# Where row stores, first weight splits and squares stand around a seven-product matmul stage

## The chip, the cores and the metric

The kernel runs on one core of one Trainium2 chip. The metric is device time in microseconds (us) of one execution, the median of several; a profile of one further execution goes with it. Each engine of the core works through a queue of its own in order: TensorE (PE, with its weight loads PEld), VectorE (DVE), ScalarE (ACT), GpSimd (POOL) and SyncE (SP), which here issues the transfers between main memory (DRAM) and the on-chip memory. Engines wait for each other by semaphores.

## The reference: what is computed

One layer of a bidirectional hybrid encoder for two requests with shared weights: 1024 rows of `x_sample` and 256 rows of `x_prompt`, each of width 2048.

```python
hn = rms_norm(x, norm_g)
proj = hn @ w_in                       # 2048 -> 4896 columns
xbc, z_ssd, dt_raw, q, k, v, z_att, mq, z_mem = split_cols(proj, IN_SIZES)
xbc = silu(centred_dwconv(xbc, conv_w, conv_b))          # 5 taps along the rows
...                                    # two SSD scans, windowed attention, attention to the memory
return x + concatenate([o_ssd, o_att, o_mem], axis=-1) @ w_out
```

The memory (2 x 256 rows of width 2048) is normed and multiplied with `w_mem_kv` in the same way. All matrices are float32.

## The kernel before

**Rows and places.** The 1280 rows are taken as two groups of 640; group 1 (rows 640 to 1279) comes first. A group lies transposed on the chip in 16 places, `xH0..xH15` and `xL0..xL15`, each of 128 features by 640 rows. Every float32 operand is held as two parts, a rounded one (H) and the rest (L), and a product is three matmuls: H by H, H by L, L by H. Weights come as tiles `wraw`, 128 x 512 (256 KB), and are split by `wsplit` (line 337): ACT copies the rounded part `wh`, then DVE subtracts to get `wl`. There are four buffers for `wraw` and three each for `wh` and `wl`. `wsplit` notes its two instructions in the list `marks`.

**Two kinds of block.** `block_tok` (line 367) multiplies 16 weight tiles with four or five tiles of rows and holds five sums in the `acc` banks of PSUM; its last pass takes k = 14 and 15 together, sum by sum, and calls `evac` for each (an ACT copy, then a store: `ev_raw` writes `qs`, `ev_kv` writes `kv`, the memory blocks `mkr` and `mvo`). `block_pair` (line 1326) is a Strassen-like form: seven products of half tiles stand for eight, each k having 21 matmuls of 320 columns. It needs sums of the quarters of the weight tile: `weight_sums` (line 1308) loads the tile and lets POOL make three sums `ws` in four instructions; these are split as well, into `sh` (ACT) and `sl` (DVE), three buffers each. Its seven results take the five `acc` banks and two more (`accm`).

**The order.** The blocks run as follows: the two memory blocks (MK, then MV), `q` of group 1, ten units of seven products for group 1 (`seven_stage(1)`, each unit with 8 values of k), `kv` and `q` of group 0, `seven_stage(0)`, and then the mixed part with the remaining blocks, the scans and the attention. The last part multiplies with `w_out`.

**What runs beside them.** `p_step` (line 1411) is called once for each k of a block and prepares the rows of a group by a plan written out by hand: `p_load` brings in two row tiles `ra` and `rb_`, `p_fill` (line 1378) scales them and writes the places (`xH` by ACT, `xL` by DVE), `p_sums` and `p_split` form and split the row sums `tH` and `tL`. For group 1 it runs beside MV, `q` and unit 0 of `seven_stage(1)`; for group 0 beside `kv`, `q` and unit 0 of `seven_stage(0)`. `p_fill` of group 1 also stores each place to DRAM, 32 stores `rowH` and `rowL` of 320 KB; `refill_x` reads them back in a `z1` block of the mixed part. At j = 23 and j = 25, k = 7 and 9 of the `q` block, `p_step` calls `weight_sums` for the first two weight tiles of the seven-product stage, into tiles that are free until then.

`stage_stats` (line 1513) is a generator of 48 steps, four for each group of three pieces: it loads pieces `sst` of rows (256 KB), squares and sums them on ACT, and after every fourth piece has DVE and POOL make the norm factor `rx`. It has one buffer, `xst`, which also serves for one of the first two weight tiles and for the sums `yu` of a unit. `seven_stage` (line 1665) takes one step at k = 0, 2, 4 and 5 of every unit: 40 in the first stage, 8 in the second. `some_left` and `one_left` work off the convolution of finished units (`u`, `c`).

**Who decides the order in a queue.** The framework sorts each engine's queue at build time by walking a model of the machine: whichever instruction is ready goes, and among ready ones the earlier in the program. `tc.high_priority(offset=n)` counts an instruction as standing n places earlier. `tc.issue_after(ins)` keeps those instructions of its block that go to the engine of `ins` behind `ins` in that engine's queue; it says nothing about other engines. The offsets are `HP = (30, 100, 100)`: evacuations of `block_tok` take the first, weight sums, splits and evacuations of `block_pair` the third.

```python
def wsplit(raw, h, l):
    a = A.activation(h, raw, AF.Copy)
    b = V.tensor_sub(l, raw, h.bitcast(F32))
    marks[:] = a.ins, b.ins
```

Of the kernel before, what the change touches and what calls it, by code (L numbers as in the profile page):

```python
# [10 lines left out]
F32 = mybir.dt.float32  # L11
# [10 lines left out]
KT = D // P  # L22
# [3 lines left out]
HP = (30, 100, 100)  # L26
# [124 lines left out]
def hymba_encoder_kernel(  # L151
# [79 lines left out]
    row_d = [[dram([P, 640], f"row{n}{k}") for n in "HL"] for k in range(KT)]  # L231
# [28 lines left out]
            lanes[lane].append(((fn.__name__, t), fn(t)))  # L260

    marks = []

    def step(i):
        name, gen = lanes[i][0]
# [45 lines left out]
    cur = {}  # L311
# [31 lines left out]
    def w_laid(src, n):  # L343

        def load(k, raw):
            S.dma_start(raw, src[k])
        return load, n

    def laid_in(name):
# [4 lines left out]
    def w_in_rows(name):  # L354
        return w_laid(laid_in(name), W_AT[name][1])
# [8 lines left out]
    TURNED = [4 * q + m for q in (0, 2, 1, 3) for m in range(4)]  # L364
    PAIRED = [k + 8 * i for k in range(8) for i in range(2)]

    def block_tok(w, nt, evac, before_last=None, feats=range(KT), places=range(KT)):

        load, n = w
        ps = [acc.tile([P, 512], F32, tag="acc", name="acc") for _ in range(nt)]  # L370
        hls = {}
        for k in range(KT):
            raw = wp.tile([P, 512], F32, tag="wraw", name="wraw", bufs=RB)
            load(feats[k], raw[:, :n])
            with tc.high_priority(offset=HP[2]):
                h = wp.tile([P, 512], F32R, tag="wh", name="wh", bufs=WB)
                l = wp.tile([P, 512], F32R, tag="wl", name="wl", bufs=WB)
                wsplit(raw[:, :n], h[:, :n], l[:, :n])
            hls[k] = h, l
            if k == KT - 2:  # L380
                continue
            if k == KT - 1 and before_last is not None:
                before_last(k)

            for t in range(nt):
                for k_ in ((k - 1, k) if k == KT - 1 else (k,)):
                    h, l = hls[k_]
                    sh, sl = [cur[n_, places[k_]][:, t * P:(t + 1) * P] for n_ in "HL"]
                    T.matmul(ps[t][:, :n], sh, h[:, :n], start=(k_ == 0), stop=False)
                    T.matmul(ps[t][:, :n], sh, l[:, :n], start=False, stop=False)  # L390
                    T.matmul(ps[t][:, :n], sl, h[:, :n], start=False, stop=(k_ == KT - 1))
                if k == KT - 1:
                    with tc.high_priority(offset=HP[0]):
                        evac(t, ps[t])
                if nt == 5 and t < 4:
                    yield 0.4 if k == KT - 1 else 0.2
            if k == KT - 1:
                yield k - 1
            yield k
# [908 lines left out]
    def weight_sums(src, i):  # L1308

        if i >= 8 * src.shape[0]:  # L1310
            return
        if i < 2 and src is w_in_pairs:
            raw = fin.tile([P, 512], F32, tag=("xst", "tL7")[i], name="wraw0")
        else:
            raw = wp.tile([P, 512], F32, tag="wraw", name="wraw", bufs=RB)
        S.dma_start(raw, src[i // 8, i % 8])
        with tc.high_priority(offset=HP[2]):
            sums = fin.tile([P, 384], F32, tag="ws", name="ws", bufs=3)
            w11, w12, w22, w21 = [raw[:, i * P:(i + 1) * P] for i in range(4)]
            s1, s2, s4 = [sums[:, i * P:(i + 1) * P] for i in range(3)]  # L1320
            for o, x, y, op in ((s1, w21, w22, ALU.add), (w21, w11, w21, ALU.subtract),
                                (s2, s1, w11, ALU.subtract), (s4, w12, s2, ALU.subtract)):
                G.tensor_tensor(out=o, in0=x, in1=y, op=op)
        ahead.append((raw, sums))

    def block_pair(src, u, rows_of, begin, lead=1):

        ps = {p: (acc.tile([P, 512], F32, tag="acc", name="acc") if i < 5 else psum("accm"))[:, :320]
              for i, p in enumerate(seven)}
        parts = {}  # L1330
        for k in range(8):
            weight_sums(src, 8 * u + k + lead)
            with tc.high_priority(offset=HP[2]):
                raw, sums = ahead.pop(0)
                h = [wp.tile([P, 512], F32R, tag="wh", name="wh", bufs=WB),
                     fin.tile([P, 384], F32R, tag="sh", name="sh", bufs=3)]
                l = [wp.tile([P, 512], F32R, tag="wl", name="wl", bufs=WB),
                     fin.tile([P, 384], F32R, tag="sl", name="sl", bufs=3)]
                wsplit(raw, h[0], l[0])
                wsplit(sums, h[1], l[1])  # L1340
            parts[k] = h, l
            if k == 2:
                evac = begin(u)
            if k == 6:
                continue
            ks = (6, 7) if k == 7 else (k,)
            for p, (i, m, c) in seven.items():
                for k_ in ks:
                    h, l = [x[i][:, m * P:(m + 1) * P] for x in parts[k_]]
                    xh, xl = rows_of(k_, p, c)  # L1350
                    T.matmul(ps[p], h, xh, start=(k_ == 0), stop=False)
                    T.matmul(ps[p], h, xl, start=False, stop=False)
                    T.matmul(ps[p], l, xh, start=False, stop=(k_ == 7))
                if k == 7:
                    with tc.high_priority(offset=HP[2]):
                        evac(p, ps[p])
            yield k
# [20 lines left out]
    def p_fill(k, grp):  # L1378

        for i, x in enumerate(raw[k]):  # L1380
            g_ = R_G + k + 8 * i
            V.scalar_tensor_tensor(out=x, in0=x, scalar=vec[:, g_:g_ + 1], in1=rbc, op0=ALU.mult, op1=ALU.mult)
            h, l = new_place(k + 8 * i)
            A.activation(h, x, AF.Copy)
            V.tensor_sub(l, x, h.bitcast(F32))
            if grp == 1:
                for d, y in zip(row_d[k + 8 * i], (h, l)):
                    S.dma_start(d, y.bitcast(F32))

    def p_sums(k):  # L1390
        a, b = [hv(x, 2) for x in raw[k]]
# [19 lines left out]
    def p_step(j, grp):  # L1411
        if j == (3, 9)[grp]:
            need(x_rows, [1 - grp])
        if j in (23, 25):
            weight_sums(w_in_pairs, (j - 23) // 2)
        with ExitStack() as st:
            for ins in marks:
                st.enter_context(tc.issue_after(ins))
            for f, k, *args in sorted(p_plan[grp].get(j, ()),
                                      key=lambda x: ((p_split, p_sums, p_fill, p_load).index(x[0]), x[1])):  # L1420
                f(k, *args)
# [99 lines left out]
    def run(gen, rates, after=None, hold=0, lag=2, extra=None):  # L1521

        begun, fine = 0, False
        for k in gen:
            if isinstance(k, float):
                fine = True
                if begun >= hold:
                    pump(part_of(rates, k))
                continue
            begun = k + 1  # L1530
            if after is not None and k % 4 == 3:
                pend.extend(after(k // 4))
            if hold:
                for _ in range(2 if k < KT - 4 else 0):
                    if pend:
                        u = pend.popleft()()
                        next(u)
                        next(u)
            else:

                if loaded and (len(loaded) == lag or not pend or k >= KT - 4):
                    next(loaded.popleft())
                if pend and k < KT - 4:
                    loaded.append(pend.popleft()())
                    next(loaded[-1])

            if k >= hold:
                pump(part_of(rates, 0.2 if fine else 1.0))
            if extra is not None:
                extra(k)  # L1550
# [103 lines left out]

    def tok(name, evac, rates=(0, 0), after=None, extra=None, paired=False):
        order = PAIRED if paired else range(KT)
        run(block_tok(w_in_rows(name), 5, evac, feats=order, places=order), rates, after, extra=extra)

    queue(0, vectors, [0])
    tok("q", ev_raw(q_d, 5), (1.0, 0), extra=lambda k: p_step(16 + k, 1), paired=True)  # L1660
# [4 lines left out]
    def seven_stage(grp):  # L1665
        owe = 0.0
        for u, unit in enumerate(units):
            for k in block_pair(w_in_pairs, u, rows_in, ev_seven(*unit, grp), lead=2):
                if k in (0, 2, 4, 5):
                    next(squares, None)  # L1670
                owe = owe + 1.15 if left else 0.0
                while owe >= 1:
                    owe -= 1
                    one_left()
                if u == 0:
                    p_step(32 + k, grp)

    def both(k, j):
        one_left()
# [180 lines left out]
```

## Time and profile before

| what | value |
|---|---|
| median of 3 runs | 1792.16 us (1790.08 to 1795.26) |
| profiled execution | 1788.47 us, its span 1786.8 us |
| PE busy | 1762.2 us, 99% of the span |
| DVE, ACT, POOL busy | 1302.3, 974.9, 668.4 us |
| moved by DMA | 313.23 MB, 175 GB/s on average |
| granted TensorE clock, mean | 0.998 |

The span runs from the first to the last instruction of the program. A row of a timeline has the start in us, the duration in us, the engine, the source line (here always that of a helper), the operation with its output and inputs, the count, and in brackets the idle time of the engine before it with what ended it. A row of the table by windows has, for each engine, the busy time and in brackets the number of instructions, then the granted clock (1.00 is full), the share of time in which the DMA engines were busy, and GB/s. Matmuls overlap, so a matmul's duration is longer than the distance from its start to the next one's start; that distance is what the array needs.

### The profile page before, as it was taken

To read this page: it belongs to the slowest core of one execution; us is meant where nothing else is said; L and a number is where in the kernel's file an instruction comes from. 1 tells how busy PE (TensorE), PEld (TensorE's weight loads), DVE (VectorE), ACT (ScalarE), POOL (GpSimd) and SP (SyncE) were. 2 spreads that over 40 slices of the span, in tenths; PEclk is the share of its full clock that TensorE was granted. 3 is DMA by queue.
4 is the path that set the end of the run, shared out by engine and by line. 5 is a ranking of instruction groups with operands and counts; after the bars stand their busy time and mean duration, and the time that the engine had idled before them with its cause. 6 is when DMAs were issued, how large, how long until landed. Compare 5 with 4: busy or idle time off the path is not lost.

```text
span 1786.8 us, 30971 instructions
## 1 busy us (share of the span) xinstructions
PE 1762.2 (99%) x10306; PEld 1574.1 (88%) x10306; DVE 1302.3 (73%) x2417; ACT 974.9 (55%) x2181; POOL 668.4 (37%) x1092
## 2 busy tenths in 40 slices
PE   9999999999999999999999999999999999999999
PEld 7778999999799999988778877877788888889999
DVE  5585788888958888787788777768776533766665
ACT  6554545554454444346778766657886533433433
POOL 0105788970158889421111001121110100058775
PEclk9999999999999999999999999999999999999999
DMA  8795454455443333366557876666885635644442
GB/s 297 236 309 177 140 140 144 127 146 180 146 148 106 103 118 109 100 200 199 155 162 243 258 248 185 218 199 221 249 254 164 207 115 149 209 136 147 148 142 78
DMA packets 210993, 313.23 MB, mean 175 GB/s; under 512 B 21584, under 2 KB 84368, under 8 KB 210832
## 3 DMA queue, kind: packets, MB, share of 16 engines
q1 hardware_dynamic: 210688, 311.19, 56.1%
q8 instruction: 81, 1.33, 0.3%
q14 instruction: 80, 0.66, 0.1%
q10 hardware_dynamic: 144, 0.06, 0.0%
HBM read 242.42 MB, written 68.75 MB: 174 GB/s over the span
## 4 chain that ended last, share of the span: by engine, by line
PE 81%; issue 6%; DMA 5%; DVE 4%; ACT 2%; POOL 1%; SPq 0%; DVEq 0%; ACTq 0%; POOLq 0%
PE acc L128 58%; PE accm L128 11%; PE py L128 2%; PE psc L128 1%; PE po L128 1%; DVE wl L128 1%; PE pst L128 1%; PE ppt L128 1%; DMA rf<-ac 1%; PE pmo L128 1%; PE pms L128 1%; PE pyf L128 1%; PE pyb L128 1%; DMA wraw<-in_w_in_pairs_dram 1%; DMA rb<-ac 0%
## 5 line engine op out<-in xcount | busy, mean ns | idle before, releaser
L128 PE MATMUL acc<-wh,xH 128*128 128x512 f32 (+1 forms) x1248 | 490.7, 394 | 4.2 <-ACT wh L128 3.7
L128 DVE TENSOR_TENSOR wl<-wraw,wh 128x512 fp32r<-128x512 f32 (+1 forms) x480 | 353.1, 740 | 173.9 <-ACT wh L128 169.8
L128 PE MATMUL acc<-wl,xH 128*128 128x512 f32 (+1 forms) x1248 | 475.1, 381 | 2.8 <-DVE wl L128 2.6
L128 PE MATMUL acc<-wh,xL 128*128 128x512 f32 (+1 forms) x1248 | 472.6, 379 | 0.0
L128 ACT ACTIVATE wh<-wraw 128x512 fp32r<-128x512 f32 (+1 forms) x480 | 291.7, 614 | 200.4 <-PE acc L128 125.7
L128 POOL TENSOR_TENSOR ws<-wraw 128x128 f32<-128x128 f32 x224 | 144.7, 646 | 400.4 <-DMA wraw<-in_w_in_pairs_dram 202.9
L128 PEld LDWEIGHTS acc<-wh,xH 128*128 128x128 f32 x1248 | 234.9, 188 | 51.1 <-issue 7.0
L128 PEld LDWEIGHTS acc<-wl,xH 128*128 128x128 f32 x1248 | 235.2, 188 | 48.7 <-issue 6.5
L128 PEld LDWEIGHTS acc<-wh,xL 128*128 128x128 f32 x1248 | 234.6, 188 | 44.5 <-issue 1.0
L128 ACT ACTIVATE sh<-ws 128x384 fp32r<-128x384 f32 x224 | 116.3, 524 | 275.6 <-POOL ws L128 132.3
L128 DVE TENSOR_TENSOR sl<-ws,sh 128x384 fp32r<-128x384 f32 x224 | 157.1, 704 | 136.8 <-ACT sh L128 134.8
L128 POOL TENSOR_TENSOR ws<-wraw,ws 128x128 f32<-128x128 f32 x224 | 153.4, 685 | 17.3
L128 POOL TENSOR_TENSOR ws<-ws,wraw 128x128 f32<-128x128 f32 x224 | 152.8, 682 | 0.0
L128 POOL TENSOR_TENSOR wraw<-wraw 128x128 f32<-128x128 f32 x224 | 134.9, 602 | 17.3
L128 PE MATMUL acc<-xH,wl 128*128 128x320 f32 x320 | 100.1, 313 | 1.7 <-DVE wl L128 1.4
L128 PE MATMUL acc<-tH,sh 128*128 128x320 f32 x320 | 99.1, 310 | 1.9 <-ACT qs L128 1.9
L128 PE MATMUL acc<-tH,sl 128*128 128x320 f32 x320 | 99.2, 310 | 0.0
L128 PE MATMUL acc<-xL,wh 128*128 128x320 f32 x320 | 98.9, 309 | 0.0
L128 PE MATMUL accm<-tH,wl 128*128 128x320 f32 x320 | 98.8, 309 | 0.0
L128 PE MATMUL acc<-xH,wh 128*128 128x320 f32 x320 | 98.7, 309 | 0.0
L128 PE MATMUL accm<-tL,wh 128*128 128x320 f32 x320 | 98.7, 308 | 0.0
L128 PE MATMUL accm<-tH,wh 128*128 128x320 f32 x320 | 98.7, 308 | 0.0
(458 smaller groups left out, 3833.0 us busy)
## 6 DMA issues: line engine op xcount, KB each, us to landing
wraw<-in_w_in_pairs_dram SPq DMA_DIRECT2D x160, 256.0 KB, 2.7
wraw<-in_w_in_laid_dram SPq DMA_DIRECT2D x128, 256.0 KB, 3.6
wraw<-in_w_out_laid_dram SPq DMA_DIRECT2D x64, 256.0 KB, 3.0
wraw<-in_w_out_pairs_dram SPq DMA_DIRECT2D x64, 256.0 KB, 2.9
rf<-ac SPq DMA_DIRECT2D x40, 256.0 KB, 3.8
rb<-ac SPq DMA_DIRECT2D x40, 256.0 KB, 4.1
wraw<-in_w_mem_laid_dram SPq DMA_DIRECT2D x32, 256.0 KB, 4.4
ra<-in_x_turned_dram SPq DMA_DIRECT2D x16, 320.0 KB, 3.2
```

Of the source, the lines that this page charges most:

```text
L128: r = f(*a, **kw)
```

## The change

Five things are edited.

1. `p_fill` no longer stores the places. A new function `keep_rows` issues one store; `seven_stage(1)` calls it at k = 0, 2, 4 and 7 of units 2 to 9, 32 times in all.
2. The loads and sums of the first two weight tiles, called at j = 23 and 25, stand in a block that queues their load behind the load of the weight tile last asked for (`raws[0]`).
3. In unit 0 of a stage the splits of k = 0, 1 and 2 (`wh`, `wl`, `sh`, `sl`) are queued on ACT and DVE behind the last split of the block in front.
4. `stage_stats` takes no step in unit 0 of either stage: 36 steps in the first stage, 12 in the second.
5. Evacuations of the blocks with `paired=True` (the two `q` blocks and the `kv` block between the seven-product stages) have the offset 100 in place of 30.

```diff
@@ step / w_laid @@
+    raws = [None]
...
-            S.dma_start(raw, src[k])
+            raws[0] = S.dma_start(raw, src[k]).ins
@@ block_tok @@
-                    with tc.high_priority(offset=HP[0]):
+                    with tc.high_priority(offset=rush):
@@ block_pair @@
+        front = tuple(marks) if u == 0 else ()
         for k in range(8):
             weight_sums(src, 8 * u + k + lead)
-            with tc.high_priority(offset=HP[2]):
+            with ExitStack() as st:
+                st.enter_context(tc.high_priority(offset=HP[2]))
+                for ins in front if k < 3 else ():
+                    st.enter_context(tc.issue_after(ins))
@@ p_fill @@
-            if grp == 1:
-                for d, y in zip(row_d[k + 8 * i], (h, l)):
-                    S.dma_start(d, y.bitcast(F32))
@@ p_step @@
-        if j in (23, 25):
-            weight_sums(w_in_pairs, (j - 23) // 2)
         with ExitStack() as st:
             for ins in marks:
                 st.enter_context(tc.issue_after(ins))
+            if j in (23, 25):
+                st.enter_context(tc.issue_after(raws[0]))
+                weight_sums(w_in_pairs, (j - 23) // 2)
@@ tok @@
-        run(block_tok(..., feats=order, places=order), rates, after, extra=extra)
+        run(block_tok(..., feats=order, places=order, rush=HP[2 * paired]), rates, after, extra=extra)
@@ seven_stage @@
-                if k in (0, 2, 4, 5):
+                if k in (0, 2, 4, 5) and u:
                     next(squares, None)
+                if grp == 1 and 2 <= u < 10 and k in (0, 2, 4, 7):
+                    keep_rows(4 * (u - 2) + (0, 2, 4, 7).index(k))
...
+    def keep_rows(i):
+        with ExitStack() as st:
+            for ins in marks:
+                st.enter_context(tc.issue_after(ins))
+            k, n = divmod(i, 2)
+            S.dma_start(row_d[k][n], cur["HL"[n], k].bitcast(F32))
```

More of the change, by code (lines that the diff above doesn't have):

```diff
@@ L365, in hymba_encoder_kernel, with block_tok @@
     PAIRED = [k + 8 * i for k in range(8) for i in range(2)]
-    def block_tok(w, nt, evac, before_last=None, feats=range(KT), places=range(KT)):
+    def block_tok(w, nt, evac, before_last=None, rush=HP[0], feats=range(KT), places=range(KT)):
         load, n = w
@@ L1656, in tok @@
         order = PAIRED if paired else range(KT)
-        run(block_tok(w_in_rows(name), 5, evac, feats=order, places=order), rates, after, extra=extra)
+        run(block_tok(w_in_rows(name), 5, evac, feats=order, places=order, rush=HP[2 * paired]), rates, after, extra=extra)
     queue(0, vectors, [0])
```

## The prediction

> **What bounds the kernel now.** First the page: which engine is busy throughout, and what the chain that ended last is made of. Then a table by windows of the places that the change touches, and last the timelines of single engines there.
>
> ```profile
> span 1786.8 us, 30971 instructions
> PE 1762.2 (99%) x10306; PEld 1574.1 (88%) x10306; DVE 1302.3 (73%) x2417; ACT 974.9 (55%) x2181; POOL 668.4 (37%) x1092
> ...
> PE 81%; issue 6%; DMA 5%; DVE 4%; ACT 2%; POOL 1%; SPq 0%; DVEq 0%; ACTq 0%; POOLq 0%
> ```
>
> PE is the bound. Work taken from another engine gains nothing; only places where PE stands still, or runs slowly, can be won. They show where a window holds fewer matmuls than an undisturbed one:
>
> ```profile
> 48.00:58.00 10.00, 8.66 (x37) 6.63 (x36) 3.79 (x5) 4.35 (x9) 4.23 (x8) 1.00 0.80 254
> 106.00:116.00 10.00, 8.53 (x38) 6.75 (x37) 5.96 (x10) 3.09 (x5) 0.00 (x0) 1.00 0.98 348
> 153.00:163.00 10.00, 8.02 (x41) 7.24 (x41) 3.92 (x7) 5.16 (x12) 2.56 (x7) 0.83 0.71 234
> 272.00:282.00 10.00, 8.63 (x59) 8.37 (x58) 9.79 (x15) 4.05 (x9) 9.45 (x14) 1.00 0.43 133
> 484.00:499.00 15.00, 12.68 (x49) 9.84 (x49) 6.84 (x10) 7.62 (x15) 8.05 (x12) 0.89 0.38 111
> 300.00:400.00 100.00, 99.67 (x681) 99.40 (x680) 86.72 (x143) 52.89 (x106) 86.93 (x131) 1.00 0.47 134
> 455.00:485.00 30.00, 30.00 (x134) 24.82 (x133) 28.09 (x47) 14.99 (x25) 2.72 (x4) 1.00 0.53 155
> ```
>
> The last two give the undisturbed distances: 100/681 = 0.147 us for 320 columns, 30/134 = 0.224 us for 512. Against them the others lose:
> - A, MK to MV (48:58): 10 - 37 x 0.224 = 1.7 us
> - B, inside `q` of group 1 (106:116): 10 - 38 x 0.224 = 1.5
> - C, `q` to `seven_stage(1)` (153:163; three of the 41 are of 512): 10 - 3 x 0.224 - 38 x 0.147 = 3.7
> - D, inside `seven_stage(1)` (272:282): 10 - 59 x 0.147 = 1.3
> - F, end of `q` of group 0 (484:499): 15 - 49 x 0.224 = 4.0
>
> A, B, C and F sum to 10.9 us. 0.3% of 1792.16 is 5.4 us, about what a measurement of this kernel can tell from no change, so the change can be seen only if it wins half of this.
>
> **Part 4, squares out of unit 0 (C).** In these timelines the bracket is the idle time before the instruction and who ended it.
>
> ```profile
> 149.82 1.06 ACT L128 ACTIVATE qs<-acc 128x512 f32<-128x512 f32 x2
> 155.15 0.63 ACT L128 ACTIVATE sst<-sst 128x512 f32<-128x512 f32 x1 [4.26 <-DMA sst<-in_x_sample_dram]
> 155.77 1.07 ACT L128 ACTIVATE qs<-acc 128x512 f32<-128x512 f32 x2
> 156.73 1.15 ACT L128 ACTIVATE wh<-wraw 128x512 fp32r<-128x512 f32 x2
> ...
> 154.25 0.31 PE L128 MATMUL acc<-xH,wl 128*128 128x320 f32 x1
> 156.40 0.55 PE L128 MATMUL acc<-tH,sh 128*128 128x320 f32 x1 [1.85 <-ACT qs L128]
> 156.75 0.47 PE L128 MATMUL acc<-tL,sh 128*128 128x320 f32 x1
> 157.02 0.47 PE L128 MATMUL acc<-tH,sl 128*128 128x320 f32 x1
> ```
>
> ACT has evacuated two sums of `q`; next in its queue is a square whose piece is still on its way. ACT stands for 4.26 us, behind it stand the evacuations that free the `acc` banks, and PE waits 1.85 us for one. Afterwards the matmuls start 0.27 us apart (156.75 to 157.02) and the clock of the window is 0.83: 3.7 - 1.85 = 1.85 us more. Without the square, the third evacuation comes at about 150.9 in place of 155.77, ahead of 154.25. Each step taken out of unit 0 is one 256 KB load, one square with its read-out and, every fourth, a reduction and two POOL instructions; all run later in the same stages under busy PE (the second stage gets 12 in place of 8): nothing. Next in line are `wh` and `wl` of k = 1, which need buffers that `q` frees at its end; PE needs them 21 x 0.147 = 3.1 us later, and a split takes 0.6 on ACT and about as much on DVE. I take all of C: 3.7.
>
> **Parts 2 and 3, first sums and splits behind the block in front (A and F).** SP and ACT around A, ACT and POOL around F:
>
> ```profile
> 41.02 0.33 SPq L128 DMA_DIRECT2D dtb<-in_dt_bias_dram  x1
> ...
> 44.45 0.43 SPq L128 DMA_DIRECT2D wraw<-in_w_in_pairs_dram  x1
> ...
> 52.00 0.53 ACT L128 ACTIVATE sh<-ws 128x384 fp32r<-128x384 f32 x1 [2.94 <-POOL ws L128]
> 52.43 1.14 ACT L128 ACTIVATE wh<-wraw 128x512 fp32r<-128x512 f32 x2
> ...
> 53.09 0.50 PE L128 MATMUL acc<-wh,xH 128*128 128x512 f32 x1 [0.65 <-ACT wh L128]
> 54.28 0.50 PE L128 MATMUL acc<-wl,xH 128*128 128x512 f32 x1 [0.69 <-DVE wl L128]
> ...
> 480.85 0.91 POOL L128 TENSOR_TENSOR ws<-wraw 128x128 f32<-128x128 f32 x1 [67.37 <-DMA wraw<-in_w_in_pairs_dram]
> ...
> 483.76 0.53 ACT L128 ACTIVATE sh<-ws 128x384 fp32r<-128x384 f32 x1 [3.28 <-POOL ws L128]
> ...
> 488.59 0.74 ACT L128 ACTIVATE tH<-rb__5692 128x640 fp32r<-128x640 f32 x1 [2.52 <-DVE rb__5692 L128]
> 489.23 1.14 ACT L128 ACTIVATE wh<-wraw 128x512 fp32r<-128x512 f32 x2
> ...
> 489.90 0.50 PE L128 MATMUL acc<-wh,xH 128*128 128x512 f32 x1 [1.62 <-ACT wh L128]
> 491.11 0.79 PE L128 MATMUL acc<-wl,xH 128*128 128x512 f32 x1 [0.70 <-DVE wl L128]
> ```
>
> At 44.45 SP loads a weight tile of the stage that begins shortly before 154.25, and at 52.00 ACT makes its `sh`, having stood 2.94 us for POOL's sums; the `wh` of MV behind it is what PE waits for. At 483.76 it is `sh` of k = 2 that stands ahead of the last `wh` of `q` and holds ACT for 3.28 us, and PE waits 1.62 and 0.70 us for `wh` and `wl`. The edit keeps these splits of k = 0 to 2 behind the last split of the block in front, so neither can precede that `wh`. I take A and F whole: 1.7 + 4.0. Their work is then due between the last split and the stage (at F from 489.23 to about 499). For k = 0 and 1 that is two `sh` on ACT (2 x 0.53), two `sl` on DVE and eight POOL instructions, one weight load each on SP behind the load of k = 7. They are covered by the ACT idle time above (4.26 at C, 2.52 at F). Uncovered, two `sh` and two `sl` at about 0.8 are 1.1 + 1.6 = 2.7 us at each of the two borders. Between 0 and 5.4 I take 2.0 given back, nearer to 0 because the idle rows stand beside it.
>
> **Part 1, the stores.** SP and ACT ahead of B:
>
> ```profile
> 78.31 0.33 SPq L128 DMA_DIRECT2D rowH<-xH  x1
> ...
> 102.30 0.33 SPq L128 DMA_DIRECT2D rowH<-xH  x1
> ...
> 105.25 0.32 SPq L128 DMA_DIRECT2D rowH<-xH  x1
> 106.11 0.32 SPq L128 DMA_DIRECT2D rowL<-xL  x1
> 106.48 0.42 SPq L128 DMA_DIRECT2D rb__1225<-in_x_turned_dram  x1
> 106.96 0.96 SPq L128 DMA_DIRECT2D wraw<-in_w_in_laid_dram  x1
> ...
> 111.71 0.63 ACT L128 ACTIVATE wh<-wraw 128x512 fp32r<-128x512 f32 x1 [3.19 <-DMA wraw<-in_w_in_laid_dram]
> ```
>
> A weight load stands behind stores that wait for `xH` and `xL`, with the DMA engines 98% busy in that window, and `wh` comes late. If the stores are gone, so is B; but the two row loads between them wait for buffers too. Between 0 and 1.5 I take half: 0.75. In their new place 32 stores of 320 KB share SP with the weight loads:
>
> ```profile
> wraw<-in_w_in_pairs_dram SPq DMA_DIRECT2D x60, 256.0 KB, 2.7
> ...
> wraw<-in_w_in_laid_dram SPq DMA_DIRECT2D x16, 256.0 KB, 3.9
> ```
>
> The first row is from 200 to 400 us, the second from 77 to 145, where the stores are now: a weight load beside stores lands 1.2 us later. From nothing to 32 x 1.2 = 38 us, I take nothing: in 300:400 the DMA engines are 47% busy and POOL, next after the load, 87%, so a landed tile stands in POOL's queue.
>
> **Part 5, evacuations.** Where `kv` meets `q`, PE waits this long for an evacuation that stands behind a split:
>
> ```profile
> PE acc L128 <- ACT kv L128: 0.4, 1, 0.4
> ```
>
> From 0 to 0.4, I take 0.2. At C and F the new offset only puts evacuations level with the splits; it is counted there.
>
> **The sum.** 1.7 + 0.75 + 3.7 + 4.0 + 0.2 - 2.0 = 8.35 us. The profiled execution took 1788.47 us, 1.67 over its span, and would take 1780.1; the median of the runs shown is 3.7 us above it, so 1792.16 - 8.35 = 1783.8. Its own range: 1780 (all of B, nothing given back) to 1787.2 (5.4 given back).
>
> **A rule weighed.** After C's wait of 1.85 us the clock row is 0.83, after F's two waits 0.89, after A's two of 0.65 and 0.69 it is 1.00: the slow stretch goes with the longer waits. [...]
>
> **Rivals.**
> - *Only the waits are won.* The slow stretch at a stage's start stays for a reason of its own. Then C gives 1.85 and F 2.32 in place of 7.7: 8.35 - 3.5 = 4.85 us, 1787.3. For it: both slow stretches lie at a border. Against it: in the border at A the clock held.
> - *The stores do not move.* `issue_after` in `keep_rows` names instructions of ACT and DVE, the store is SP's, and SP's queue is sorted by readiness: `dtb` above is loaded at 41.02, though its step stands in the `q` block, all of MV later. The first row is ready by 78.31. Then B stays and stage 1 is free of stores: 1783.8 + 0.75 = 1784.6.
> - *The border stays crowded.* Splits and evacuations, all at offset 100, meet on ACT in that time; 2.7 us come on PE's path at both borders and bring the slow stretch of about 1.85 each: what is won before anything is given back, 8.35 + 2.0 = 10.35 us, shrinks by 2 x 4.55 to 1.25, 1790.9.
> - *Slower: stores in front of weight loads.* In units 2 to 9 every store delays a load, POOL's sums and PE. D shows the chain: POOL is busy for 9.45 of 10 us there and PE loses 1.3 us. With 10.35 us won elsewhere, it decides from 10.35/32 = 0.32 us a store; at 0.5 us, under half of the 1.2 above, 16 - 10.35 = 5.65 slower, 1797.8.
>
> **How the numbers follow.** Forecast 0.38, stores not moved 0.25, crowded 0.20, slower 0.09, only waits 0.08. Forecast and unmoved stores lie below 1786.8, nearly all faster by over 0.3%: 0.61 with their upper edge and a few of the others set off. Crowded and only-waits are within 0.3%, with that edge 0.30; slower 0.09. The range drops the slower case and reaches to the crowded one, 1791; downward it takes D as well (1.3) and the runs' own spread of about 2 us below a median: 1777.
>
> **What would show it.** In the changed trace: no `sh` on ACT before the last `wh` of `q`; no idle ACT for `sst` between evacuations at C; PE without waits at 52, 154 and 488 and the clock 1.00 there; `rowH` and `rowL` on SP between 200 and 405 if they moved, between 78 and 145 if not. The prediction is wrong if a new PE wait for `qs`, `wh` or `sl` stands at a border, or if waits for `sh` or `sl` follow stores inside the stage.

## The result, and the profile after

The changed kernel takes 1774.85 us (median of 4 runs, 1773.83 to 1778.13) against 1792.94 for the kernel before on the same chip: a ratio of 0.9903, interval 0.9883 to 0.9923. A second comparison gave 1776.25 against 1790.24, 0.9921 (0.9909 to 0.9934). The change is faster by 0.8 to 1.0%, 14 to 18 us. The forecast was 1783.8 with a range from 1777 to 1791: the sign was right, the gain was 1.7 to 2.2 times the 8.35 us of the sum, and the time lies below the range in both comparisons.

The page of the profile after (profiled execution 1773.83 us):

```profile
span 1772.1 us, 30974 instructions
PE 1755.3 (99%) x10306; PEld 1572.0 (89%) x10306; DVE 1310.9 (74%) x2417; ACT 971.8 (55%) x2181; POOL 683.8 (39%) x1092
...
PE 88%; DMA 4%; DVE 3%; ACT 2%; issue 1%; POOL 1%; SPq 0%; ACTq 0%; DVEq 0%; POOLq 0%
```

The span is 14.7 us shorter with the same 10306 matmuls. In the chain that ended last PE has 88% where it had 81%, and "issue" 1% where it had 6%: PE stands still less often. The table by windows shows where. The borders here are the first matmuls of the blocks; the rows are the memory blocks with `q` of group 1, `seven_stage(1)`, `q` of group 0, and the mixed part. Before:

```profile
5.40:153.50 148.10, 144.96 (x636) 118.32 (x635) 95.18 (x152) 79.56 (x147) 16.50 (x31) 1.00 0.82 275
153.50:405.80 252.30, 248.62 (x1682) 247.24 (x1681) 202.64 (x331) 129.53 (x260) 204.15 (x314) 0.99 0.48 140
...
439.10:498.70 59.60, 56.90 (x243) 46.09 (x242) 48.95 (x76) 30.45 (x50) 10.77 (x16) 0.97 0.56 166
...
777.80:1583.90 806.10, 798.40 (x4230) 651.90 (x4229) 572.01 (x1251) 515.50 (x1325) 88.10 (x164) 1.00 0.64 199
```

After:

```profile
5.40:149.00 143.60, 143.50 (x636) 118.34 (x635) 96.90 (x152) 81.51 (x150) 25.62 (x34) 1.00 0.85 289
149.00:396.10 247.10, 246.44 (x1681) 245.90 (x1680) 203.22 (x330) 125.96 (x252) 201.96 (x309) 1.00 0.47 137
...
428.80:483.20 54.40, 54.40 (x242) 45.06 (x241) 52.82 (x78) 30.11 (x50) 19.78 (x22) 1.00 0.58 179
...
762.60:1570.00 807.40, 798.21 (x4231) 652.21 (x4230) 572.82 (x1252) 514.06 (x1325) 87.82 (x164) 1.00 0.64 199
```

The second number of a row is the length of the block. The first block lost 4.5 us, the first stage 5.2, the `q` block of group 0 5.2; `kv` ahead of it (33.3 to 32.7 between these borders) 0.6. All that comes later is 0.8 us longer in sum (the mixed part alone 1.3). The windows of 10 us at the five places A, B, C, D and F, each shifted about as far as its block (the last is 15 us):

```profile
48.00:58.00 10.00, 10.00 (x46) 8.29 (x45) 2.15 (x4) 4.91 (x12) 0.74 (x2) 1.00 0.81 262
106.00:116.00 10.00, 10.00 (x46) 8.29 (x45) 10.00 (x15) 5.56 (x10) 9.77 (x7) 1.00 0.94 316
149.00:159.00 10.00, 10.00 (x70) 9.99 (x69) 8.46 (x13) 5.96 (x11) 5.28 (x8) 1.00 0.37 116
267.00:277.00 10.00, 9.96 (x68) 9.97 (x69) 9.46 (x15) 5.40 (x11) 9.45 (x15) 1.00 0.41 104
468.50:483.50 15.00, 15.00 (x68) 12.44 (x67) 13.14 (x18) 8.57 (x15) 10.62 (x15) 1.00 0.38 125
```

A holds 46 matmuls in place of 37 (9 x 0.224 = 2.0 us), B 46 in place of 38 (1.8 us), C none too few, D 68 in place of 59 (9 x 0.147 = 1.3 us), F 68 in place of 49 (19 x 0.224 = 4.3 us). The granted clock is 1.00 in all five. All five losses are gone, D among them, which the forecast had left standing, and no new one stands beside them.

One thing did not happen: the stores did not move. Transfers issued by SP between 77 and 145 us in the kernel after, with the time from issue to landing:

```profile
rowH<-xH SPq DMA_DIRECT2D x15, 320.0 KB, 4.5
rowL<-xL SPq DMA_DIRECT2D x15, 320.0 KB, 4.9
```

The other two lie just outside this window; from 185 to 400 us there is none. What changed is the order in SP's queue (timeline of SP after):

```profile
97.50 0.38 SPq L128 DMA_DIRECT2D ra<-in_x_turned_dram  x1
98.18 0.33 SPq L128 DMA_DIRECT2D rb__1209<-in_x_turned_dram  x1
98.56 2.14 SPq L128 DMA_DIRECT2D wraw<-in_w_in_laid_dram  x3
100.75 0.44 SPq L128 DMA_DIRECT2D wraw<-in_w_in_pairs_dram  x1
101.23 0.43 SPq L128 DMA_DIRECT2D rowL<-xL  x1
```

Row loads and weight loads now stand ahead of a store that once stood ahead of them. What that saves shows in the waits of SP's queue from 77 to 145 us (total, times, longest). Before:

```profile
SPq L128 <- ACT xH L128: 17.0, 13, 2.2
SPq L128 <- DVE xL L128: 6.4, 13, 0.9
```

After:

```profile
SPq L128 <- DVE wl L128: 13.3, 14, 1.6
...
SPq L128 <- ACT xH L128: 1.1, 2, 0.7
```

For 23.4 us SP stood before a store whose `xH` or `xL` was not written yet, with loads behind it, some of which could have gone: for the weight load at 106.96 us, the one that B waits for, the buffers were free by 102.17 us, when DVE's last split before B ended. Now that is 1.1 us. SP waits for `wl` instead (13.3 us in place of 3.2), that is for a free `wraw` buffer, and for `tL` (10.1 in place of 4.4), that is for a free row buffer: the loads are as far ahead as the buffers allow.

### The profile page after: what moved, and what is told of

It is laid out like the page before. It is cut to its first block, busy times and chain, and to the rows that moved or that the text cites. A ratio compares the mean times of both kernels' runs of the same rounds, so it can differ in the third digit from the quotient of the medians.

```text
span 1772.1 us, 30974 instructions
## 1 busy us (share of the span) xinstructions
PE 1755.3 (99%) x10306; PEld 1572.0 (89%) x10306; DVE 1310.9 (74%) x2417; ACT 971.8 (55%) x2181; POOL 683.8 (39%) x1092
## 4 chain that ended last, share of the span: by engine, by line
PE 88%; DMA 4%; DVE 3%; ACT 2%; issue 1%; POOL 1%; SPq 0%; ACTq 0%; DVEq 0%; POOLq 0%
PE acc L128 66%; PE accm L128 11%; PE py L128 2%; PE po L128 1%; PE psc L128 1%; PE pst L128 1%; PE pmo L128 1%; PE pms L128 1%; PE ppt L128 1%; DMA wraw<-in_w_in_laid_dram 1%; PE pyf L128 1%; DMA xst<-in_x_prompt_dram 1%; DVE wl L128 1%; PE pyb L128 0%; ACT lg L128 0%
## 5 line engine op out<-in xcount | busy, mean ns | idle before, releaser
L128 POOL TENSOR_TENSOR ws<-wraw 128x128 f32<-128x128 f32 x224 | 156.9, 700 | 365.8 <-DMA wraw<-in_w_in_pairs_dram 163.1
L128 DVE TENSOR_TENSOR sl<-ws,sh 128x384 fp32r<-128x384 f32 x224 | 158.7, 712 | 115.4 <-ACT sh L128 113.9
L128 POOL TENSOR_TENSOR wraw<-wraw 128x128 f32<-128x128 f32 x224 | 139.8, 624 | 17.1
```

Of the source, the lines that this page charges most:

```text
L128: r = f(*a, **kw)
```

## The experiments

Parts are numbered as in the change. Ratios are against the kernel before, on the same chip.

**Parts 2 and 3 alone.** The kernel before with `weight_sums` of j = 23 and 25 behind `raws[0]`, and the splits of k < 3 of unit 0 behind `marks`.

> Before with parts 2 and 3 alone (first two weight loads behind the block's loads, splits of k = 0 to 2 behind the last split of the block in front). Border theory (each part takes away the waits of its own border, and the parts add up): the waits at 52 us (A) and 488 us (F) go with the slow stretch after F, 1.9 + 4.4 = 6.3 us less than before; the wait at 154 us (C) and that at 111 us (B) stay. Rival 'queue order on SP' (the gain is the row stores' lower rank behind weight loads): under 2 us. Rival 'crowded border': the splits that now come late take the place of the waits, under 3 us, with PE waits for sh, sl or wh at 154 and 498.

1783.62 us, 0.9966 (0.9953 to 0.998). The waits for `wh` and `wl` at A and F are gone but for 0.2 us; but from 100 to 160 us PE waits more than before:

```profile
PE acc L128 <- ACT wh L128: 2.9, 3, 1.8
PE acc L128 <- ACT qs L128: 1.2, 2, 0.8
PE acc L128 <- DVE wl L128: 0.5, 2, 0.2
```

The two loads of the seven-product weights are now late in the `q` block, in a queue that still stands before the stores. From 100 to 150 us PE does 201 matmuls, against 214 before and 224 with the whole change: parts 2 and 3 without part 1 cost 13 x 0.224 = 2.9 us there. At the second border, where the kernel before has no wait for `qs`, there is one now (470 to 500 us):

```profile
PE acc L128 <- ACT qs L128: 1.1, 2, 0.8
```

With F gone PE comes to this border earlier, and ACT stands 1.42 us for the piece of a square with two evacuations behind it; in the kernel before it stood 0.33 us there.

**Part 4 alone.** The kernel before with no step of `stage_stats` in unit 0:

```diff
-                if k in (0, 2, 4, 5):
+                if k in (0, 2, 4, 5) and u:
```

> Before with part 4 alone (no step of the squares in unit 0). Border theory: the wait at 154 us (C) and its slow stretch go, 3.9 us less than before; A, B and F stay. Rival 'queue order on SP': nothing. Rival 'next in line' (wh or sh of unit 0 is late as well): under 1.5 us, with a PE wait for wl or sl shortly after 154.

1788.97 us, 0.9992 (0.9979 to 1.0004). C is gone. What is left of the PE waits from 100 to 160 us is B, in the profiled execution longer than before (2.0 us in place of 1.5) and with a slow stretch behind it (clock 0.83 from 113.9 to 123.9 us), so that little gain is left: the median is 1.9 us lower, and the interval takes in no change.

**Part 1 alone.** The kernel before with the stores out of `p_fill` and `keep_rows` in the stage.

> Before with part 1 alone (the stores in keep_rows). In the changed kernel's trace the stores are issued from 76 to 140 us, as before from 78 to 141, only behind more of the weight loads. Border theory: only B goes, 1.8 us less than before, and the stores are issued up to about 141 us here too. Rival 'queue order on SP': with the weight loads in front, the waits of the memory and q blocks and some of those at the borders go, 5 us or more.

1783.61 us, 0.9969 (0.9956 to 0.9983). The stores again go out from 79 to 139 us, and the view of waits has not one row for PE from 100 to 160 us: B is gone, and so is C, although the squares are where they were. ACT at the border:

```profile
148.35 0.60 ACT L128 ACTIVATE qs<-acc 128x512 f32<-128x512 f32 x1 [0.76 <-PE acc L128]
150.42 0.63 ACT L128 ACTIVATE sst<-sst 128x512 f32<-128x512 f32 x1 [1.48 <-DMA sst<-in_x_sample_dram]
...
151.05 1.07 ACT L128 ACTIVATE qs<-acc 128x512 f32<-128x512 f32 x2
```

The square still stands ahead of two evacuations, but its piece arrives after 1.48 us of idle ACT and not after 4.26.

**Part 5 alone.** `block_tok` with `rush=HP[2 * paired]`, else the kernel before.

> Before with part 5 alone (evacuations of the paired blocks at offset 100). Border theory: only the wait of 0.4 us for an evacuation between kv and q goes, 0 to 0.7 us less than before. Rival: the evacuations now pass the square at 154 us (C) on ACT as well, 3.9 us less, and part 4 is not needed.

1791.9 us, 1.0007 (0.9997 to 1.0017): only the wait of 0.4 us for `kv` at the start of `q` of group 0 was at stake. It is gone, which cannot be measured in the time. At C the square still comes first on ACT (4.15 us idle), and waits of 1.4 us for `qs` are left.

**The change without part 1.** The stores back in `p_fill`.

> The changed kernel with part 1 undone: p_fill stores the places again. Theory 'rank' (the stores stay beside the q block and only stand behind the weight loads in SP's queue, which spares q of group 1 its waits for wh): 4 to 6 us slower than the changed kernel, about 1780 beside a before of 1791, with PE waits for wh between 105 and 150. Theory 'border' of the prediction: 1.8 us slower, one wait near 111.

1783.21 us, 0.9957 (0.9945 to 0.9969). The block of memory and `q` takes 149.15 us, 5.5 more than with part 1, the first stage 249.14, 2.0 more:

```profile
5.40:154.55 149.15, 145.68 (x636) 118.58 (x635) 97.47 (x151) 79.48 (x147) 19.51 (x32) 1.00 0.80 276
154.55:403.69 249.14, 247.24 (x1682) 245.97 (x1680) 203.95 (x331) 127.58 (x255) 204.30 (x311) 1.00 0.44 137
```

Within the whole change part 1 is worth 7.5 us by these two rows, 6.4 or 9.7 us by the ratios (0.9957 against 0.9921 or 0.9903, of 1791 us): about half of the gain, ten times the term of the forecast. Not all of this was there in the kernel before: from 100 to 150 us PE does 201 matmuls here as with parts 2 and 3 alone, so that 2.9 us of the loss come only with parts 2 and 3, most likely by part 2's loads in the same queue.

**The change without part 4, and without parts 2 and 3.** In each the named parts are undone.

> The changed kernel with part 4 undone: four steps of the squares in unit 0 of either stage. With part 1 alone the wait at 154 was gone although the squares stayed. Theory 'the squares matter only while the stores hold up SP': within 1 us of the changed kernel. Theory 'border': 3.9 us slower, a PE wait for qs at the start of the stage.

1776.45 us, 0.9917 (0.9904 to 0.993), as with part 4: with parts 1 and 5 there it adds nothing that can be measured.

> The changed kernel with parts 2 and 3 undone. Theory 'border': A and F come back, with A's 2.3 and F's 2.0 of waits in the traces of the kernels that lack these parts: 4.3 us slower than the changed kernel, and up to 6.5 where the slow clock follows F. Rival 'the other parts cover it': under 2 us.

1785.97 us, 0.9972 (0.9963 to 0.9981). Within the change parts 2 and 3 are thus worth 9.1 or 12.4 us (against 0.9921 or 0.9903), more than the 4.3 to 6.5 expected and no less than part 1. A and F are back, with their waits and, at F, the slow stretch (matmuls 0.42 us apart where 0.227 is the undisturbed distance); the profile is of the slowest run, 1790.52 us:

```profile
53.90 0.51 PE L128 MATMUL acc<-wh,xH 128*128 128x512 f32 x1 [1.46 <-ACT wh L128]
55.10 0.50 PE L128 MATMUL acc<-wl,xH 128*128 128x512 f32 x1 [0.70 <-DVE wl L128]
...
483.61 0.50 PE L128 MATMUL acc<-wh,xH 128*128 128x512 f32 x1 [1.95 <-ACT wh L128]
484.81 0.79 PE L128 MATMUL acc<-wl,xH 128*128 128x512 f32 x1 [0.71 <-DVE wl L128]
485.41 0.63 PE L128 MATMUL acc<-wh,xL 128*128 128x512 f32 x1
485.83 0.63 PE L128 MATMUL acc<-wh,xH 128*128 128x512 f32 x1
```

**Part 2 undone, part 5 undone, and the change once more.**

> The changed kernel with part 2 undone: the first two weight tiles of the stage are loaded and summed as early as before (44 to 55 us), part 3 still keeps their splits late. Theory 'splits': A and F came from the splits alone, so this is within 1 us of the changed kernel. Rival 'loads': the early loads or POOL's sums were part of A, 1 to 2 us slower, with a PE wait near 52.

1777.37 us, 0.9927 (0.9914 to 0.994). A and F stay away: the splits alone (part 3) remove them, and the interval overlaps with the change's, so that part 2 adds nothing that can be measured. One wait of 0.9 us for `wh` is new in MV.

> The changed kernel with part 5 undone (evacuations of the paired blocks at offset 30). Theory 'border': with parts 2 and 3 alone PE waited 1.2 and 1.1 us for qs at the two borders; either of parts 4 and 5 may have taken that away. If part 5 did: 1.5 to 2.5 us slower than the changed kernel, with waits for qs and kv. If part 4 did: within 1 us.

1775.77 us, 0.9919 (0.9906 to 0.9932), no different from the change.

> The changed kernel once more, beside the others on one chip: ratio 0.990 (0.988 to 0.992), the clock 1.0 or 0.999 in every run, a spread under 5 us. Theory 'slow clock' (before loses some 2 to 7 us a run to slow stretches that follow its waits, by chance of the moment): the runs of before lie the higher the lower their clock, about 1.6 us for each 0.001.

1776.25 us, the second comparison above.

**Is it the place of the stores?** The changed kernel, with each store of `keep_rows` also queued on SP behind the pair load last issued:

```diff
-        S.dma_start(raw, src[i // 8, i % 8])
+        pairs[0] = S.dma_start(raw, src[i // 8, i % 8]).ins
...
+            st.enter_context(tc.issue_after(pairs[0]))
             k, n = divmod(i, 2)
```

> The changed kernel with each store of keep_rows queued on SP behind the pair load last issued in the program, so that the stores really go out in units 2 to 9. Theory 'rank': the q block is already free of waits, so nothing more is won: within 1 us of the changed kernel, stores between 200 and 400 us. Rival 'stores in front of weight loads' (the prediction's slower case): a store holds up a weight load, POOL's sums and PE, 0.3 us each or more: 5 to 16 us slower, PE waits for sl or wl in the stage. Rival 'less traffic in q': 1 to 2 us faster.

Now the stores did move, to 190 to 379 us. The time is 1774.46 us, 0.9909 (0.9894 to 0.9923): the same. Windows of the `q` block and of the stage in this kernel:

```profile
100.00:150.00 50.00, 50.00 (x224) 41.50 (x223) 41.54 (x64) 24.22 (x40) 19.46 (x24) 1.00 0.51 158
200.00:380.00 180.00, 179.29 (x1220) 178.35 (x1219) 156.83 (x248) 93.67 (x189) 161.02 (x239) 1.00 0.62 196
```

and in the changed kernel:

```profile
100.00:150.00 50.00, 50.00 (x224) 41.54 (x224) 41.62 (x63) 24.27 (x41) 21.74 (x24) 1.00 0.90 315
200.00:380.00 180.00, 179.34 (x1223) 178.81 (x1222) 155.67 (x248) 93.82 (x189) 159.94 (x239) 1.00 0.50 144
```

The DMA engines go from 90% to 51% busy beside `q` and from 50% to 62% in the stage, and PE does the same 224 matmuls in the one and, within 3, as many in the other. Neither the traffic beside `q` nor the stores beside the stage's weight loads cost PE anything that these counts or the time show.

**Is it the rank?** The change without part 1, with the stores in `p_fill`, but the weight loads of the paired blocks given an earlier rank; then the row loads as well:

```diff
-            load(feats[k], raw[:, :n])
+            with tc.high_priority(offset=400 if rush == HP[2] else 0):
+                load(feats[k], raw[:, :n])
@@ p_load, second kernel only @@
-            S.dma_start(raw[k][i], x_turned[grp, r * P:(r + 1) * P, :])
+            with tc.high_priority(offset=400):
+                S.dma_start(raw[k][i], x_turned[grp, r * P:(r + 1) * P, :])
```

> The changed kernel with part 1 undone (p_fill stores the places) but the weight loads of the q and kv blocks counted as 400 places earlier. The stores keep their place and their amount; only the rank of the weight loads in SP's queue is raised. Theory 'rank': the waits between 105 and 150 us go as with keep_rows, ratio about 0.991, 1 to 2 us from the changed kernel. Rival 'traffic' (the 10 MB of stores beside the loads are what costs): as with part 1 undone, ratio 0.9957, waits for wh near 109 and 142.

1782.5 us, 0.9954 (0.9942 to 0.9967). From 100 to 150 us PE does 220 matmuls, against 201 without the new rank: 4.3 us won there, and no wait for `wh` is left. SP's waits for `xH` and `xL` are still 17.1 us, and the row loads still stand behind stores; waits for `qs` came back, 1.6 us in two.

The whole time did not follow the 4.3 us: it is that of the change without part 1, and the rival 'traffic' had forecast this ratio. In the profile 1.8 went in the mixed part, whose program is the same. So this run bears the rank out for the waits for `wh`, not for the whole price.

> As loads_first (stores in p_fill, parts 2 to 5 as in the changed kernel), with the row loads of p_load counted 400 places earlier too. Theory 'rank': SP's waits for xH no longer hold up anything, ratio 0.990 to 0.992 as in the changed kernel, no PE wait between 100 and 155. Rival 'traffic': the stores' amount beside the loads costs, ratio stays at 0.995.

1782.5 us, 0.9947 (0.9934 to 0.996). From 100 to 170 and from 470 to 500 us no PE wait is left, with the stores where they were before the change, the DMA engines 94% busy, more than in any other kernel here, and SP's waits for `xH` and `xL` down to 3.1 us:

```profile
100.00:150.00 50.00, 50.00 (x222) 41.41 (x221) 40.75 (x67) 23.34 (x39) 5.31 (x11) 1.00 0.94 327
```

For the waits that is rank, not traffic. The time missed its expectation and is where the rival had it. The trace shows a reason that the edit itself made: row loads now also pass the weight loads of MK, ACT stands 8.15 us for a weight tile there, and PE waits.

```profile
35.41 0.79 PE L128 MATMUL acc<-wh,xH 128*128 128x512 f32 x1 [2.28 <-ACT wh L128]
```

```profile
36.00:46.00 10.00, 10.00 (x32) 7.88 (x32) 3.01 (x6) 5.48 (x14) 0.76 (x2) 0.70 0.71 220
```

With the window ahead of it (26:36, 33 matmuls) that is 65 matmuls in 20 us where the changed kernel has 92: 27 x 0.224 = 6.0 us of the 7.5 that part 1 is worth: the edit moved the loss to the front. A wait of 1.4 us for `kv` at 440 us is new too. That the time would be the changed kernel's without these two is worked out from the trace; no run shows it. (The first stage, 247.49 us between its borders, is as short as with the change.)

**Do parts 4 and 5 cover each other?** The change with both undone.

> The changed kernel with parts 4 and 5 both undone. Theory 'either covers the other': one of them alone was enough at the borders, without both PE waits for qs at 150 and 484, 1 us each as with parts 2 and 3 alone, ratio 0.993 to 0.995. Rival 'neither is needed once the stores no longer hold up SP': ratio 0.990 to 0.992.

1778.38 us, 0.9928 (0.9913 to 0.9944). Waits for `qs` are back at both borders; the rows are from 100 to 170 us and from 470 to 500 us:

```profile
PE acc L128 <- ACT qs L128: 0.6, 1, 0.6
...
PE acc L128 <- ACT qs L128: 1.1, 2, 0.8
```

Undoing part 4 alone left 0.3 us of them at the second border, undoing part 5 alone left none. The intervals of the ratios overlap with the change's, so that the cover shows in the waits, not in the time.

## Why the prediction was wrong

| step | forecast, us | profile after, us |
|---|---|---|
| A, MK to MV | 1.7 | 2.0 |
| B, inside `q` of group 1 | 0.75 | 1.8 |
| rest of memory and `q` | 0 | 0.7 |
| C, start of `seven_stage(1)` | 3.7 | 3.9 |
| D and the rest of the stage | 0 | 1.3 |
| `kv` to `q`, and F | 0.2 + 4.0 | 0.6 + 5.2 |
| given back at the two borders | -2.0 | 0 |
| all later blocks | 0 | -0.8 |
| sum | 8.35 | 14.7 |

The sum fell 6.35 us short of the 14.7 in the profile (C is what the first stage won less D). The step that failed is the sizing of the sum's terms; the places and most of the mechanism were right. Most went wrong at four terms: 2.0 us were to be given back and none were; B and the rest of its block, priced at 0.75, held 2.5; `kv` to F held 5.8 in place of 4.2; and D, 1.3 us, was left standing. A and C held 0.5 more, and the later blocks cost 0.8. The median fell 2.7 us further: the forecast kept the 3.7 us by which the median of the kernel before stood above its profiled execution, and after the change that distance is 1.0 us (1774.85 against 1773.83). Which run is profiled is chance; that slow stretches behind waits are gone (the mean granted clock is 0.999 or 1.0 in the four runs after, and went from 0.996 to 0.999 in 27 runs of the kernel before) would make the distance smaller too, but this is not shown apart. The sum's own lower edge, given as 1780, is 1781.1 by its terms (1792.16 - 8.35 - 0.75 - 2.0), still above the result.

*Part 1: the term that failed most, by parts.* The prediction saw the mechanism (a weight load behind stores that wait for `xH`) and priced it at the one PE wait it could see, half of 1.5 us. Done alone, it gains 5.6 us by its ratio (0.9969); undone, it costs about 7.5, 2.9 of them by way of parts 2 and 3. A queue that stands for 23.4 of 68 us delays other loads too, and the delay shows at another place under another name: the pieces `sst` come later (4.26 us of idle ACT in place of 1.48), and C is a wait for `qs` behind the late square. The rival "the stores do not move" was right about the place, and right about why: `issue_after` on ACT's and DVE's instructions binds nothing on SP. Its price was wrong ("then B stays"): a store that is asked for later loses its rank to loads that are ready, and that was enough to free PE of its waits: with part 1 alone SP's waits for `xH` and `xL` fell from 23.4 to 7.2 us, and PE has none from 100 to 160 us.

*Part 4: right place, but not part 4's alone.* C has two sufficient removals: without the square (part 4 alone) or with its piece in time (part 1 alone). In the full change either would do. Its 3.7 us were rightly counted once, but neither part can be credited with them, and this swap between parts did not move the sum.

*Parts 2 and 3: right place, too small.* A and F were to be won whole, and were; undone, they come back. Part 3 alone does it. With 1.7 + 4.0 won and 2.0 given back they were to bring 3.7 us net; by place A and `kv` to F brought 7.8, and undoing them costs 9.1 or more. Parts 2 and 3 without part 1 leave waits of 4.6 us from 100 to 160 us, where the kernel before has 3.4. The product of the four ratios of single parts is 0.9966 x 0.9992 x 0.9969 x 1.0007 = 0.9934, against 0.9903 and 0.9921 for the whole: the parts seem to help each other, but the intervals touch, so that this is only indicated.

*The 2.0 us given back did not come,* and the rival of the crowded border is refuted for the whole change. With parts 2 and 3 alone waits for `qs` of 1.2 and 1.1 us stood at the two borders, the second of them new, and with parts 4 and 5 undone 0.6 and 1.1: what the term feared was there, but as late evacuations, and either of parts 4 and 5 takes away nearly all of it, which the sum did not count. The late splits themselves cost nothing that the trace shows: the three `sh` fit between the last splits of `q`, where ACT was idle before and after them (timeline of ACT after):

```profile
139.00 0.63 ACT L128 ACTIVATE wh<-wraw 128x512 fp32r<-128x512 f32 x1 [2.72 <-PE acc L128]
139.54 1.34 ACT L128 ACTIVATE sh<-ws 128x384 fp32r<-128x384 f32 x3
142.40 0.63 ACT L128 ACTIVATE wh<-wraw 128x512 fp32r<-128x512 f32 x1 [1.52 <-PE acc L128]
```

*The slower rival fell by the run with moved stores:* 32 of them beside the stage's weight loads left 0.7 us of PE waits from 150 to 400 us, as many as in the changed kernel. *Only the waits are won* fell too: with the waits gone, the clock is 1.00 at C and F.

*Open:* D, 1.3 us, which no step of the prediction touched, went away as well, and this was luck. From 200 to 380 us PE does 1215 matmuls before and 1223 after, but 1222 with part 4 alone, 1224 without parts 2 and 3, and 1212 without part 5, whose time is the change's; no part can be credited, and no run isolates why. Nor is it explained why the mixed part, the same program in all, varies from 805 to 811 us over the profiles. A kernel without any row stores was not tried, since the mixed part reads them back.

## What to carry to other kernels

When an in-order queue issues both loads and stores, read its own waits first: price a store by the time the queue stands before it for its producer and by everything queued behind, not by the one PE wait beside it (here 23.4 of 68 us against a wait of 1.5). To defer a store, it was enough here to let it be asked for later than the loads that could go (23.4 us of SP's waits became 7.2 with part 1 alone); check in the queue's timeline where it really went, since an ordering on another engine's instruction bound nothing here: 30 of the 32 stores went out between 77 and 145 us, ahead of the stage that calls for them. And if a loss has two sufficient removals, undo each part of the change by itself before crediting either.

## What the hardware showed that was not expected

Slow stretches of the array (at F in the kernel before, matmuls 0.42 us apart in place of 0.227) came after waits shorter than the stretch (at C 1.85 us, then 3.5 us from 156.40 to 159.92), and the length of the wait alone did not decide. After 1.85 us (C) the clock of the window was 0.83, after 2.28 us (all loads first) 0.70; after 1.79 us in the kernel with parts 2 and 3 alone it stayed full:

```profile
143.50:153.50 10.00, 9.95 (x44) 8.25 (x45) 8.94 (x12) 4.84 (x10) 8.34 (x13) 1.00 0.34 112
```

These three would fit a limit between 1.79 and 1.85 us. But with part 4 alone two shorter waits at F did bring it, the matmuls then 0.42 us apart:

```profile
487.60 0.49 PE L128 MATMUL acc<-wh,xH 128*128 128x512 f32 x1 [1.30 <-ACT wh L128]
488.80 0.50 PE L128 MATMUL acc<-wl,xH 128*128 128x512 f32 x1 [0.71 <-DVE wl L128]
...
489.68 0.63 PE L128 MATMUL acc<-wl,xH 128*128 128x512 f32 x1
490.10 0.63 PE L128 MATMUL acc<-wh,xL 128*128 128x512 f32 x1
```

The waits of 1.46 and 0.70 us at A without parts 2 and 3, shown above, are in sum longer (2.16 us against 2.01), and behind them the matmuls soon start 0.23 us apart again. So something besides the length of the waits counts; what it is, no run shows. A stretch lasted about 3.5 us (before, at F, 491.11 to 494.59; with part 4 alone, at B, 113.94 to 117.44) or 6.1 to 6.7 us (without parts 2 and 3, at F, 484.81 to 490.95, the clock 0.69 from 484.8 to 494.8; all loads first, 35.41 to 42.13, the clock 0.70 from 36 to 46).

The mean granted clock of one kernel differs from run to run, and the average time goes with it. Of 27 runs of the kernel before on one chip, five with a mean granted clock of 0.996 took 1793.1 us on average, four with 0.997 1791.7, thirteen with 0.998 1790.1, and five with 0.999 1788.3: about 1.6 us for each 0.001, where 0.001 of the whole time is 1.8 us. Since a wait cost its own length and sometimes about as much again (at C 1.85 us and 1.85 more), a kernel without waits should also be the steadier one: five runs of the change's repeat lie within 1.9 us (1775.69 to 1777.63), the eleven of the kernel before on the same chip within 7.1 (1787.17 to 1794.31), though with so few runs this is only indicated.
